# A wide S5 recurrence, a bound state copy, a diagonal skip on TensorE, and S5 outputs' DMAs on other queues

## Chip, cores and metric

One core of one Trainium2 chip runs the whole program in one launch. The metric is device time in microseconds (us), the median of the runs. Engines: TensorE (PE; PEld is its weight load), VectorE (DVE), ScalarE (ACT), GpSimd (POOL), SyncE (SP); SP's instructions are nearly all DMA issues.

## What is computed

Two layers of a hybrid block over 512 latent and 256 context tokens, width 1024. In each layer a token mixer joins three parts, then comes a gated FFN. The parts that the change touches, cut from the reference:

```python
def ssd_mixer(...):                       # width 256, 4 heads of 64
    y_l = d * x_l                         # the skip: d has one value per head
    for direction in range(2):
        yl_d, _ = ssd_scan(...)
        y_l = y_l + o(yl_d)
    return rmsnorm(y_l * silu(z_l), norm_w)

def s5_scan(u, ab, bb, h0):               # complex, 16 groups of 64 states, 16 channels a group
    h[t] = ab * h[t - 1] + bb @ u[t]      # written as an associative scan
def s5_mixer(...):                        # both directions, context then latent
    y = d * u + c_re @ h_re - c_im @ h_im
    y = gelu(y)
    return y * sigmoid(y @ glu_w + glu_b)
```

Differential attention (4 heads) is the third part. The last layer needs no outputs for the context tokens.

## The kernel before

Products in full precision are three fp32r products of high and low halves (L145 to L147). A layer runs its input products, the mixer (SSD, attention and S5 side by side), the output product and 22 blocks of the FFN. Each part is a Python generator, and the main function takes them forward in turns; a scheduler then fixes the order of instructions on each engine. An engine takes its own queue strictly in that order.

S5 works on chunks of 8 tokens: 96 chunks, 32 of the context and 64 of the latents. `SH` holds the states at the chunk borders, 128 partitions (64 states, forward on partitions 0 to 63, backward on 64 to 127) by real and imaginary part, 16 groups (2 x 8) and 96 columns. `s5_inputs` (L662) fills the columns with each chunk's own contribution, eight q at a time: SP loads of `Uq` (L699) and `Iq`, products (L677), ScalarE copies (L679 to L681). Then GpSimd runs the recurrence over the 96 columns, 95 steps of three instructions: L689 multiplies the last column by the powers of A (`s5t`), L691 adds the two halves (`s5u`), L692 adds that to the column. It is a generator, so SSD and attention work is queued between its steps.

`s5_outputs` (L702) runs over eight q. It loads `TO` (L708, L710) and `Uq` (L699) on SP, copies the states into `Iq` (VectorE L719 for the forward half, GpSimd L722 for the reversed one), multiplies (L726, L728), copies the result to `Yq` on ScalarE (L729) and stores it with SP (L731). `TO` and `Iq` have two buffers each. Then `gl` and `fu` are loaded (L738, L740), and the gelu, the gate's product (weights L752) and the gate follow.

In SSD, `scores` (L943) prepares one 128-token tile: GpSimd multiplies the tile by the skip weights (L976, `xdd`), VectorE adds that (L978) and the two directions (L979). `outputs` (L982) adds the within-chunk products (L986). `finish` (L990) gates, takes the reciprocal root of the mean square on GpSimd (L177 and L179, `rv` and `rr`), and scales by it on VectorE (L997). Layer 0 has six such tiles, layer 1 four.

Of the kernel before, what the change touches and what calls it, by code (L numbers as in the profile page):

```python
# [10 lines left out]
AF = mybir.ActivationFunctionType  # L11
# [13 lines left out]
NCH = CH_C + CH_L  # L25
# [30 lines left out]
HO = 1  # L56
F1 = 1
FL2 = 1
AE = 0
NB = 4  # L60
NM0 = 0
NM1 = 1
# [31 lines left out]
class Kern:  # L94
# [567 lines left out]
    def s5_inputs(self, l, P1):  # L662

        nc = self.nc

        SH = self.t(P1, [128, 2, 2, 8, NCH], "SH", bufs=1)
        self.SH = SH
        nc.gpsimd.memset(SH[:, :, :, :, 0:1], 0.0)
        for q in range(8):
# [12 lines left out]
            yield  # L682
        A = self.s5A[l].rearrange("p o i g q -> p o i (g q)")
        col = lambda k: SH[:, :, :, :, k].rearrange("p r g q -> p r (g q)")
        eng = nc.gpsimd
        yield
        for k in range(1, NCH):
            tt = self.sm(64, tag="s5t").rearrange("p (o i x) -> p o i x", o=2, i=2)
            eng.tensor_mul(tt, A, col(k - 1)[:, None].to_broadcast([128, 2, 2, 16]))  # L689
            u = self.sm(32, tag="s5u").rearrange("p (o x) -> p o x", o=2)  # L690
            eng.tensor_add(u, tt[:, :, 0], tt[:, :, 1])  # L691
            eng.tensor_add(col(k), col(k), u)  # L692
            if k % 5 == 0:
                yield

    def load_u(self, l, q, P1):
        U = self.t(P1, [128, 2, NCH], "Uq")
        for g in range(2):
            self.nc.sync.dma_start(U[:, g], self.ud[l][2 * q + g].rearrange("c j k -> j c k"))  # L699
        return U  # L700

    def s5_outputs(self, l, P1, P3, need_ctx):  # L702
# [99 lines left out]
    def ssd(self, l, P1, need_ctx):  # L802
# [99 lines left out]
        nc.tensor.matmul(cs[:, 1], self.m_ge, dA[:, :, 4:8], start=True, stop=True)  # L902
        tot = ps[:, 48:96].rearrange("p (d t h) -> p d t h", d=2, t=6)
        for d in range(2):
            nc.tensor.matmul(tot[:, d], self.ones, dA[:, :, d * 4:d * 4 + 4], start=True, stop=True)
        ac = self.t(P1, [128, 96], "acs", bufs=1)
        nc.scalar.copy(ac, ps[:, :96])
        eac = self.t(P1, [128, 2, 6, 4], "eac", bufs=1)
# [30 lines left out]
            yield  # L939
        toks = list(range(6 if need_ctx else TL))  # L940

        def scores(t):

            tok = slice(t * 128, (t + 1) * 128)
# [24 lines left out]
            for d in range(2):  # L969
                for g in range(2):  # L970
# [273 lines left out]
    def run(self):  # L1244
        tc, nc, I = self.tc, self.nc, self.I
        from contextlib import ExitStack
        with ExitStack() as es:
# [29 lines left out]
            self.ones = c([128, 128], "ones")  # L1277
            nc.vector.memset(self.ones, 1.0)
# [410 lines left out]
```

## Time and profile before

| | |
|---|---|
| median of 3 runs | 1928.36 us (1927.61 to 1930.28) |
| profiled execution | 1933.37 us, span 1931.6 us |
| busy: TensorE, VectorE, ScalarE, GpSimd | 1721.8, 1209.1, 735.6, 613.1 us |
| mean granted TensorE clock | 0.947 of full speed |

The span is the time from the first to the last instruction. A row of the busy time by window gives the window, its length, then the busy time (and instruction count) of PE, PEld, DVE, ACT and POOL, the granted TensorE clock, the DMA share and GB/s. A timeline row gives start, duration, engine, line, operation and tiles; what stands in brackets is the idle time of the engine before it and who ended it. A row of waits gives the sum, how many, and the longest. A price row gives the least, median and largest duration in ns, and the first and last start.

### The profile page before, as it was taken

Reading aid. Unit: us, or ns where it says so; the run is one execution under the profiler, and the core shown is the slowest. Engines: PE = TensorE matmul, PEld = TensorE weight load, DVE = VectorE, ACT = ScalarE, POOL = GpSimd, SP = SyncE. Lnnn points to the kernel's source line nnn. Section 1 sums busy time; section 2 is a strip of 40 time slices with the busy share of each in tenths; the row PEclk is TensorE's granted clock in tenths of the full one; section 3 lists DMA queues with packets and bytes.
Section 4 is the critical chain, followed back from the end, with each engine's and each line's share of the span. In section 5 each row is a group of like instructions: output and inputs, shape, how many; then the busy total and the mean of one; then the engine's idle time right before and its main releaser. Section 6 shows DMA issues by size and latency. Waiting matters only on the chain.

```text
span 1931.6 us, 26164 instructions
## 1 busy us (share of the span) xinstructions
PE 1721.8 (89%) x9485; PEld 1461.7 (76%) x9485; DVE 1209.1 (63%) x2212; ACT 735.6 (38%) x1375; POOL 613.1 (32%) x1027
## 2 busy tenths in 40 slices
PE   6989971886899899999999997998588999999998
PEld 1779861684788788888778887897477788888886
DVE  7877963875569456666556557657457464555555
ACT  3443420664444443322122235544346454232322
POOL 4436887120233644412600024088701210000002
PEclk8999995897999899999999998999799999999999
DMA  8464472454452333444533433452284343232322
GB/s 311 145 182 167 160 201 64 101 144 135 138 170 93 104 126 131 134 134 132 163 119 123 148 112 128 128 154 96 61 206 106 131 153 109 82 115 77 120 77 87
DMA packets 128818, 254.41 MB, mean 132 GB/s; under 512 B 42609, under 2 KB 65713, under 8 KB 128689
## 3 DMA queue, kind: packets, MB, share of 16 engines
q1 hardware_dynamic: 125312, 249.57, 41.5%
q10 hardware_dynamic: 3376, 3.17, 0.5%
q8 instruction: 75, 1.23, 0.3%
q14 instruction: 55, 0.44, 0.1%
HBM read 213.53 MB, written 41.16 MB: 132 GB/s over the span
## 4 chain that ended last, share of the span: by engine, by line
PE 49%; POOL 19%; DMA 11%; DVE 9%; issue 5%; ACT 4%; SPq 2%; POOLq 0%; DVEq 0%; ACTq 0%
POOL s5t L689 5%; PE pl L147 5%; PE pl L145 5%; PE pl L146 5%; POOL SH L692 4%; POOL s5u L691 4%; PE pc L146 3%; PE pc L147 3%; PE pc L145 3%; PE ma L145 3%; PE ma L146 3%; PE ma L147 3%; PE pp L146 3%; PE pp L145 3%; PE pp L147 3%
## 5 line engine op out<-in xcount | busy, mean ns | idle before, releaser
L140 DVE TENSOR_TENSOR lo<-raw,hi 128x1024 fp32r<-128x1024 f32 (+2 forms) x190 | 243.9, 1287 | 195.3 <-ACT hi L139 192.8
L139 ACT CAST hi<-raw 128x1024 fp32r<-128x1024 f32 (+2 forms) x190 | 197.4, 1042 | 440.2 <-PE pl L146 127.7
L147 PE MATMUL pl<-Hl,lo 128*128 128x512 f32 (+1 forms) x560 | 215.1, 384 | 10.0 <-DVE lo L140 10.0
L145 PE MATMUL pl<-Hl,hi 128*128 128x512 f32 (+1 forms) x560 | 215.6, 385 | 4.8 <-DVE xt L246 4.0
L177 POOL TENSOR_SCALAR rv<-ss 128x1 f32<-128x1 f32 x51 | 19.0, 373 | 629.0 <-ACT junk L185 627.0
L146 PE MATMUL pl<-Hl,hi 128*128 128x512 f32 (+1 forms) x560 | 214.1, 382 | 0.0
L1180 DVE TENSOR_TENSOR y<-y,ma 128x512 f32<-128x512 f32 x160 | 106.6, 683 | 87.4 <-PE ma L147 87.2
L145 PE MATMUL ma<-hi,ahi 128*128 128x512 f32 x360 | 141.7, 394 | 4.3 <-DVE y L1180 4.2
L146 PE MATMUL ma<-lo,ahi 128*128 128x512 f32 x360 | 140.8, 391 | 0.0
L147 PE MATMUL ma<-hi,alo 128*128 128x512 f32 x360 | 140.3, 390 | 0.0
L352 DVE SCALAR_TENSOR_TENSOR modj<-raw,crow 128x1024 bf16<-128x1024 f32 x56 | 72.6, 1297 | 92.9 <-DMA raw<-in_modw 92.5
L147 PEld LDWEIGHTS pl<-Hl,lo 128*128 128x128 f32 x560 | 107.0, 191 | 30.9 <-DVE lo L140 11.4
L145 PEld LDWEIGHTS pl<-Hl,hi 128*128 128x128 f32 x560 | 107.1, 191 | 23.9 <-issue 4.2
L692 POOL TENSOR_TENSOR SH<-SH,s5u 128x32 f32<-128x32 f32 x190 | 83.1, 438 | 126.5 <-ACT SH L680 112.1
L146 PEld LDWEIGHTS pl<-Hl,hi 128*128 128x128 f32 x560 | 107.2, 191 | 18.5
L145 PE MATMUL pp<-Hl,hi 128*128 128x512 f32 (+1 forms) x256 | 97.4, 383 | 13.8 <-ACT cvt L816 6.2
L145 PE MATMUL pc<-Hc,hi 128*128 128x256 f32 x352 | 99.7, 284 | 0.7 <-DVE de L395 0.7
L146 PE MATMUL pc<-Hc,hi 128*128 128x256 f32 x352 | 100.1, 284 | 0.2 <-DVE Hc L217 0.2
L147 PE MATMUL pc<-Hc,lo 128*128 128x256 f32 x352 | 99.8, 284 | 0.0
L146 PE MATMUL pp<-Hl,hi 128*128 128x512 f32 (+1 forms) x256 | 96.7, 378 | 0.5 <-DVE Hl L217 0.4
L147 PE MATMUL pp<-Hl,lo 128*128 128x512 f32 (+1 forms) x256 | 96.2, 376 | 0.5 <-DVE lo L140 0.5
L689 POOL TENSOR_TENSOR s5t<-s5A,SH 128x64 f32<-128x64 f32 x190 | 91.3, 481 | 14.3
(474 smaller groups left out, 4643.3 us busy)
## 6 DMA issues: line engine op xcount, KB each, us to landing
raw<-in_modw SPq DMA_DIRECT2D x56, 512.0 KB
raw<-in_wg SPq DMA_DIRECT2D x44, 512.0 KB
raw<-in_wu SPq DMA_DIRECT2D x44, 512.0 KB
raw<-in_wd SPq DMA_DIRECT2D x44, 512.0 KB
raw<-in_winf SPq DMA_DIRECT2D x28, 512.0 KB
modw<-in_modw SPq DMA_DIRECT2D x24, 512.0 KB
modw<-in_modwn SPq DMA_DIRECT2D x16, 512.0 KB
raw<-in_wout SPq DMA_DIRECT2D x16, 512.0 KB
```

The lines of the kernel that those rows point to most:

```text
L139: nc.scalar.copy(hi[:, :cols], raw[:, :cols])
L140: (eng or nc.vector).tensor_sub(lo[:, :cols], raw[:, :cols], hi[:, :cols].bitcast(F32))
L145: mm(out, lhs[0], rhs[0], start=first, stop=False)
L146: mm(out, lhs[0], rhs[1], start=False, stop=False)
L147: mm(out, lhs[1], rhs[0], start=False, stop=last)
L177: self.nc.gpsimd.tensor_scalar(v, ss, scale, eps, op0=ALU.mult, op1=ALU.add)
L352: ins = nc.vector.scalar_tensor_tensor(jk, w, 1.0, row[:, 0], op0=ALU.mult, op1=ALU.mult, accum_out=o[:, 0:1])
L689: eng.tensor_mul(tt, A, col(k - 1)[:, None].to_broadcast([128, 2, 2, 16]))
L691: eng.tensor_add(u, tt[:, :, 0], tt[:, :, 1])
L692: eng.tensor_add(col(k), col(k), u)
L1180: nc.vector.tensor_add(y[:, t, c], y[:, t, c], pb[h])
```

## The change

1. GpSimd's recurrence becomes wide. The powers A^2, A^4 and A^8 are made by 14 small instructions. Three levels up add neighbours at distances 1, 2 and 4 columns (`sweep`: one multiplication L709 and one addition L710 for each output part, input part and, where there are over 24 columns, half of the groups). A serial middle of 11 steps (columns 8, 16, ... 88) uses A^8, and three levels down fill the other columns. Per layer that is 64 wide instructions and 33 small ones where there were 285. The wide temporaries are `Iq` buffers.
2. The forward state copy (L753 now, L719 before) is bound to its place in program order on VectorE.
3. The skip is a product on TensorE: `DI`, the identity scaled by each head's weight (four ScalarE instructions per layer), times the tile, four 128x64 products that open `outputs`. The GpSimd product and the VectorE addition go. The sum over a chunk uses the two triangle masks in two products in place of a matrix of ones.
4. The S5 outputs' loads (TO, Uq, gl, fu, gate weights) are issued by GpSimd, their stores by ScalarE. `s5_inputs` keeps SP.

```diff
         for q in range(8):
-            U = self.load_u(l, q, P1)
+            U = self.load_u(l, q, P1, nc.sync)
...
-        for k in range(1, NCH):
+        def sweep(n, src, dst, m):
+            for o in range(2):
+                for i in range(2):
+                    w = 8 if m > 24 else 16
+                    for g in range(0, 16, w):
+                        x = slice(g, g + w)
+                        t = self.t(P1, [128, 2, 2, 128], "Iq", bufs=IQ).rearrange("p g r n -> p (g r n)")
+                        t = t[:, :w * m].rearrange("p (x k) -> p x k", x=w)
+                        eng.tensor_mul(t, X[:, i, x, src], AP[n][:, o ^ i, x, None].to_broadcast([128, w, m]))
+                        (eng.tensor_sub if o < i else eng.tensor_add)(X[:, o, x, dst], X[:, o, x, dst], t)
+                    yield
+        e = NCH
+        for n in range(3):
+            h = 1 << n
+            yield from sweep(n, slice(h, e - 2 * h, 2 * h), slice(2 * h, e, 2 * h), e // (2 * h) - 1)
+        for k in range(8, e, 8):
             tt = self.sm(64, tag="s5t").rearrange("p (o i x) -> p o i x", o=2, i=2)
-            eng.tensor_mul(tt, A, col(k - 1)[:, None].to_broadcast([128, 2, 2, 16]))
+            eng.tensor_mul(tt, A8, col(k - 8)[:, None].to_broadcast([128, 2, 2, 16]))
             u = self.sm(32, tag="s5u").rearrange("p (o x) -> p o x", o=2)
             eng.tensor_add(u, tt[:, :, 0], tt[:, :, 1])
             eng.tensor_add(col(k), col(k), u)
+        for n in reversed(range(3)):
+            h = 1 << n
+            yield from sweep(n, slice(0, e, 2 * h), slice(h, e, 2 * h), e // (2 * h))
...
-            nc.sync.dma_start(TO[:, :256].rearrange("p (g x) -> p g x", g=2), self.Td[l][:, 2 * q:2 * q + 2])
+            nc.gpsimd.dma_start(TO[:, :256].rearrange("p (g x) -> p g x", g=2), self.Td[l][:, 2 * q:2 * q + 2])
...
-            U = self.load_u(l, q, P1)
+            U = self.load_u(l, q, P1, nc.gpsimd)
...
-            ef(S[f, :, :, c0:], SH[f, :, :, q, c0:])
+            self.tc.keep_in_program_order(ef(S[f, :, :, c0:], SH[f, :, :, q, c0:]))
...
-                nc.sync.dma_start(self.yd[l][2 * q + g].rearrange("c j k -> j c k")[:, :, c0:], yb[:, g, c0:])
+                nc.scalar.dma_start(self.yd[l][2 * q + g].rearrange("c j k -> j c k")[:, :, c0:], yb[:, g, c0:])
...
-            sk = self.t(P1, [128, 256], "xdd")
-            nc.gpsimd.tensor_mul(sk, xB[:, t, :256], prm[:, 16:272])
-            ae = nc.gpsimd if AE else nc.vector
-            ae.tensor_add(yt[:, 1], yt[:, 1], sk)
-            ae.tensor_add(yt[:, 0], yt[:, 0], yt[:, 1])
+            nc.vector.tensor_add(yt[:, 0], yt[:, 0], yt[:, 1])
...
+            for h in range(4):
+                nc.tensor.matmul(yp[:, h * 64:(h + 1) * 64], DI[:, h], xB[:, t, h * 64:(h + 1) * 64], start=h == 0, stop=False)
```

VectorE in layer 0, where the state copy stood (`qkvt` is the rotary work of attention, `cv` and `gm` the SSD gates, `modj` the modulation). Before:

```order
L949 TENSOR_TENSOR gm_3628<-ma_3626,cst 128x512 [waits PE_49]
L352 SCALAR_TENSOR_TENSOR modj_3357,modc_112<-modw_3355,crow_1166 128x1024 [waits DMAHW4_49,DVE_49]
L1567 TENSOR_TENSOR qkvt_3586<-qkvt_3586,rope 128x512 [waits DMAHW7_49,DMAHW0_49,Activation_49]
L719 COPY Iq_4280<-SH_1369 64x384 [waits Pool_49]
L719 COPY Iq_4352<-SH_1369 64x384
L1566 TENSOR_TENSOR ropet_3588<-ropet_3588,rope 128x512 [waits Activation_49]
L965 TENSOR_TENSOR cv_3639<-cv_3639,gm_3628 128x512 [waits DVE_49,Activation_49]
```

And now, the same place, and, 26 rows behind L1602, the first row that waits for GpSimd:

```order
L988 TENSOR_TENSOR gm_3328<-ma_3326,cst 128x512 [waits PE_49]
L351 SCALAR_TENSOR_TENSOR modj_3019,modc_110<-modw_3017,crow_1164 128x1024 [waits DMAHW0_49,DVE_49]
L1602 TENSOR_TENSOR qkvt_3281<-qkvt_3281,rope 128x512 [waits DMAHW4_49,DMAHW3_49,Activation_49]
L1601 TENSOR_TENSOR ropet_3283<-ropet_3283,rope 128x512 [waits Activation_49]
L1004 TENSOR_TENSOR cv_3339<-cv_3339,gm_3328 128x512 [waits DVE_49,Activation_49]
...
L1031 SCALAR_TENSOR_TENSOR xdd_3592<-xdd_3592,z_1900 128x256 [waits DVE_49,Activation_49]
L1034 TENSOR_SCALAR yt_3357<-yt_3357,rr_665_3417 128x256 [waits Pool_49]
```

The two copies are gone from between the rotary work; the first stands 127 rows after L1602, among the output product's rows.

GpSimd in layer 1, around the first reciprocal root of the SSD. Before, it lies between steps of the recurrence:

```order
L692 TENSOR_TENSOR SH_11512<-SH_11512,s5u_12918 128x32 [waits Pool_49]
L177 TENSOR_SCALAR rv_2723_13232<-ss_13229 128x1 [waits Activation_49]
L689 TENSOR_TENSOR s5t_12921<-s5A_115,SH_11512 128x64 [waits Pool_49]
L179 TENSOR_TENSOR rr_2724_13234<-rv_2723_13232,mhalf 128x1 [waits Pool_49]
L691 TENSOR_TENSOR s5u_12923<-s5t_12921 128x32 [waits Pool_49]
```

And now, behind its last row, with the S5 outputs' loads after the four:

```order
L710 TENSOR_TENSOR SH_11218<-SH_11218,Iq_12838 128x384 [waits Pool_49]
L756 COPY Iq_13354<-SH_11218 64x4x64 [waits Pool_49]
L176 TENSOR_SCALAR rv_2444_12605<-ss_12602 128x1 [waits Activation_49,Pool_49]
L178 TENSOR_TENSOR rr_2445_12607<-rv_2444_12605,mhalf 128x1 [waits Pool_49]
...
L742 DMA TO_13347<-Td_81 128x256 [waits DMASW1_49,DVE_49,PE_49]
L744 DMA TO_13347<-Od_79 64x2x256 [waits DMASW2_49]
```

All four pairs of roots moved behind the recurrence and one copy.

GpSimd in layer 0, one q of the S5 outputs, where only the copies and the roots of attention (`oss`) were before:

```order
L733 DMA Uq_4111<-ud_72 128x1x96 [waits DMASW4_49,PE_49]
L733 DMA Uq_4111<-ud_72 128x1x96 [waits DMASW5_49]
L742 DMA TO_4107<-Td_80 128x256 [waits DMASW6_49,PE_49]
L744 DMA TO_4107<-Od_78 64x2x256 [waits DMASW7_49]
L744 DMA TO_4107<-Od_78 64x2x256 [waits DMASW0_49]
L756 COPY Iq_4114<-SH_1367 64x4x32 [waits DVE_49]
L756 COPY Iq_4114<-SH_1367 64x4x64
L176 TENSOR_SCALAR rv_892_4192<-oss_4026 128x2 [waits Activation_49,Pool_49]
```

Five loads per q stand in GpSimd's queue now, ahead of the copies and of attention's root.

## Rows read from the trace of the kernel before

**Rows 1.** The page: shares of the span of the chain that ended last, by engine.

```profile
PE 49%; POOL 19%; DMA 11%; DVE 9%; issue 5%; ACT 4%; SPq 2%; POOLq 0%; DVEq 0%; ACTq 0%
```

**Rows 2.** Busy time by window.

```profile
160.00:277.00 117.00, 114.08 (x793) 104.22 (x794) 101.72 (x212) 40.71 (x73) 103.80 (x166) 0.99 0.53 174
277.00:322.00 45.00, 0.83 (x2) 0.00 (x0) 0.29 (x2) 2.32 (x7) 35.86 (x122) 0.54 0.26 55
397.00:433.00 36.00, 33.61 (x254) 31.71 (x254) 29.84 (x65) 23.56 (x71) 11.02 (x19) 0.95 0.57 162
1255.00:1330.00 75.00, 73.70 (x523) 65.61 (x521) 53.26 (x130) 32.54 (x56) 63.26 (x148) 1.00 0.47 146
1330.00:1395.00 65.00, 38.61 (x234) 32.01 (x233) 27.46 (x49) 22.31 (x59) 53.73 (x150) 0.80 0.15 48
1396.00:1515.00 119.00, 103.55 (x654) 93.36 (x653) 78.75 (x139) 63.85 (x157) 9.39 (x14) 0.93 0.59 149
```

**Rows 3.** Timeline of POOL, three places.

```profile
160.28 0.67 POOL L692 TENSOR_TENSOR SH<-SH,s5u 128x32 f32<-128x32 f32 x1 [43.37 <-ACT SH L680]
...
321.95 6.03 POOL L722 COPY Iq<-SH 64x256 f32<-64x256 f32 x2
...
1255.23 0.28 POOL L692 TENSOR_TENSOR SH<-SH,s5u 128x32 f32<-128x32 f32 x1 [68.77 <-ACT SH L680]
```

**Rows 4.** Timeline of DVE in layer 0.

```profile
276.39 0.82 DVE L1567 TENSOR_TENSOR qkvt<-qkvt,rope 128x512 f32<-128x512 f32 x1
321.92 0.62 DVE L719 COPY Iq<-SH 64x384 f32<-64x384 f32 x2 [44.71 <-POOL SH L692]
...
344.13 0.35 DVE L997 TENSOR_SCALAR yt<-yt,rr 128x256 f32<-128x256 f32 x1
```

**Rows 5.** Waits of DVE from 1255 to 1420, of PE from 1320 to 1400.

```profile
DVE yt L997 <- POOL rr L179: 21.7, 4, 10.2
DVE yt L978 <- POOL xdd L976: 10.2, 1, 10.2
...
PE ma L1002 <- DVE yt L997: 17.0, 3, 7.8
PE ma L971 <- DVE gm L949: 6.7, 1, 6.7
```

**Rows 6.** Durations by line, ns min/median/max, over the whole span.

```profile
L689 POOL TENSOR_TENSOR s5t<-s5A,SH x190: 348/358/1418, 114.6 to 1391.0; 128x64 f32<-128x64 f32 x190
...
L691 POOL TENSOR_TENSOR s5u<-s5t x190: 250/253/1263, 115.8 to 1391.4; 128x32 f32<-128x32 f32 x190
...
L692 POOL TENSOR_TENSOR SH<-SH,s5u x190: 266/274/1352, 160.3 to 1392.1; 128x32 f32<-128x32 f32 x190
...
L601 POOL TENSOR_TENSOR s5x<-stag,stbg x20: 722/774/1822, 24.9 to 948.7; 128x256 f32<-128x256 f32 x20
...
L356 POOL TENSOR_TENSOR raw<-raw,crow x24: 2349/2407/3259, 576.1 to 799.0; 128x1024 f32<-128x1024 f32 x24
...
L986 PE MATMUL mb<-xdt,cv x160: 217/275/474, 323.8 to 1384.7; 128*128 128x64 f32 x160
```

**Rows 7.** Groups of POOL from 160 to 325.

```profile
L691 POOL TENSOR_TENSOR s5u<-s5t 128x32 f32<-128x32 f32 x94 | 40.7, 433 | 7.4
```

**Rows 8.** Timeline of DVE in layer 1.

```profile
1352.06 0.48 DVE L979 TENSOR_TENSOR yt<-yt 128x256 f32<-128x256 f32 x1
1362.77 0.35 DVE L997 TENSOR_SCALAR yt<-yt,rr 128x256 f32<-128x256 f32 x1 [10.23 <-POOL rr L179]
```

**Rows 9.** Durations of DMA issues by line, ns min/median/max.

```profile
L580 ACTq DMA_DIRECT2D Id<-s5is x8: 326/326/345, 67.2 to 95.2; - x8
...
L699 SPq DMA_DIRECT2D Uq<-ud x64: 574/597/738, 115.1 to 1469.5; - x64
...
L731 SPq DMA_DIRECT2D yd<-Yq x32: 572/596/650, 403.1 to 1480.8; - x32
```

**Rows 10.** The S5 output products of layer 1.

```profile
L728 PE MATMUL mb<-Iq,TO x64: 275/275/421, 1406.3 to 1479.5; 128*128 128x64 f32 x64
```

More of the change, by code (lines that the diff above doesn't have):

```diff
@@ L58 @@
 FL2 = 1
-AE = 0
 NB = 4
@@ L668, in s5_inputs @@
         nc.gpsimd.memset(SH[:, :, :, :, 0:1], 0.0)
+        eng = nc.gpsimd
+        A = self.s5A[l].rearrange("p o i g q -> p o i (g q)")
+        pw = self.t(P1, [128, 2, 2, 16], "s5pw", bufs=1)
+        A8 = self.t(P1, [128, 2, 2, 16], "s5A8", bufs=1)
+        AP = [A[:, :, 0], pw[:, 0], pw[:, 1]]
+        for a0, a1 in zip(AP, AP[1:] + [A8[:, :, 0]]):
+            t = self.sm(64, tag="s5t").rearrange("p (n x) -> p n x", n=4)
+            eng.tensor_mul(t[:, :2], a0, a0)
+            eng.tensor_sub(a1[:, 0], t[:, 0], t[:, 1])
+            eng.tensor_mul(t[:, 2], a0[:, 0], a0[:, 1])
+            eng.tensor_add(a1[:, 1], t[:, 2], t[:, 2])
+        eng.tensor_copy(A8[:, 1, 1], A8[:, 0, 0])
+        eng.tensor_scalar(A8[:, 0, 1], A8[:, 1, 0], -1.0, 0.0, op0=ALU.mult, op1=ALU.add)
         for q in range(8):
-            U = self.load_u(l, q, P1)
+            U = self.load_u(l, q, P1, nc.sync)
             Iq = self.t(P1, [128, 2, 2, 128], "Iq", bufs=IQ)
@@ L682, in s5_inputs @@
             yield
-        A = self.s5A[l].rearrange("p o i g q -> p o i (g q)")
-        col = lambda k: SH[:, :, :, :, k].rearrange("p r g q -> p r (g q)")
-        eng = nc.gpsimd
+        X = SH.rearrange("p r g q k -> p r (g q) k")
+        col = lambda k: X[:, :, :, k]
         yield
-        for k in range(1, NCH):
+        def sweep(n, src, dst, m):
[14 more added lines that the diff above has]
+        for k in range(8, e, 8):
             tt = self.sm(64, tag="s5t").rearrange("p (o i x) -> p o i x", o=2, i=2)
-            eng.tensor_mul(tt, A, col(k - 1)[:, None].to_broadcast([128, 2, 2, 16]))
+            eng.tensor_mul(tt, A8, col(k - 8)[:, None].to_broadcast([128, 2, 2, 16]))
             u = self.sm(32, tag="s5u").rearrange("p (o x) -> p o x", o=2)
@@ L692, in s5_inputs, with load_u @@
             eng.tensor_add(col(k), col(k), u)
-            if k % 5 == 0:
+            if k % 24 == 0:
                 yield
-    def load_u(self, l, q, P1):
+        for n in reversed(range(3)):
+            h = 1 << n
+            yield from sweep(n, slice(0, e, 2 * h), slice(h, e, 2 * h), e // (2 * h))
+    def load_u(self, l, q, P1, eng):
         U = self.t(P1, [128, 2, NCH], "Uq")
         for g in range(2):
-            self.nc.sync.dma_start(U[:, g], self.ud[l][2 * q + g].rearrange("c j k -> j c k"))
+            eng.dma_start(U[:, g], self.ud[l][2 * q + g].rearrange("c j k -> j c k"))
         return U
@@ L737, in s5_outputs @@
             y = self.t(P3, [128, Q, NCH], "gl", bufs=2)
-            nc.sync.dma_start(y[:, :, c0:], self.yd[l][i * 8:(i + 1) * 8].rearrange("g c j k -> (g c) j k")[:, :, c0:])
+            nc.gpsimd.dma_start(y[:, :, c0:], self.yd[l][i * 8:(i + 1) * 8].rearrange("g c j k -> (g c) j k")[:, :, c0:])
             u = self.t(P3, [128, Q, NCH], "fu")
-            nc.sync.dma_start(u[:, :, c0:], self.ud[l][i * 8:(i + 1) * 8].rearrange("g c j k -> (g c) j k")[:, :, c0:])
+            nc.gpsimd.dma_start(u[:, :, c0:], self.ud[l][i * 8:(i + 1) * 8].rearrange("g c j k -> (g c) j k")[:, :, c0:])
             yv, uv = y[:, :, c0:], u[:, :, c0:]
@@ L751, in s5_outputs @@
         gw = self.t(P3, [128, 2, 256], "gluw", bufs=1)
-        nc.sync.dma_start(gw, self.I["gluw"][l])
+        nc.gpsimd.dma_start(gw, self.I["gluw"][l])
         for m in range(2):
@@ L904, in ssd @@
         for d in range(2):
-            nc.tensor.matmul(tot[:, d], self.ones, dA[:, :, d * 4:d * 4 + 4], start=True, stop=True)
+            nc.tensor.matmul(tot[:, d], self.m_ge, dA[:, :, d * 4:d * 4 + 4], start=True, stop=False)
+            nc.tensor.matmul(tot[:, d], self.m_lt, dA[:, :, d * 4:d * 4 + 4], start=False, stop=True)
         ac = self.t(P1, [128, 96], "acs", bufs=1)
@@ L940, in ssd @@
         toks = list(range(6 if need_ctx else TL))
+        DI = self.t(P1, [128, 4, 128], "DI", bufs=1)
+        for h in range(4):
+            nc.scalar.activation(DI[:, h], self.ident, AF.Copy, scale=prm[:, 16 + h * 64:17 + h * 64])
         def scores(t):
@@ L974, in scores, with outputs @@
                                  eac[:, :, t, :, None].to_broadcast(shp))
-            sk = self.t(P1, [128, 256], "xdd")
-            nc.gpsimd.tensor_mul(sk, xB[:, t, :256], prm[:, 16:272])
-            ae = nc.gpsimd if AE else nc.vector
-            ae.tensor_add(yt[:, 1], yt[:, 1], sk)
-            ae.tensor_add(yt[:, 0], yt[:, 0], yt[:, 1])
+            nc.vector.tensor_add(yt[:, 0], yt[:, 0], yt[:, 1])
             return Es, xd, yt[:, 0]
-        def outputs(Es, xd, yt):
+        def outputs(t, Es, xd, yt):
             yp = self.bank("mb")
+            for h in range(4):
+                nc.tensor.matmul(yp[:, h * 64:(h + 1) * 64], DI[:, h], xB[:, t, h * 64:(h + 1) * 64], start=h == 0, stop=False)
             for d in range(2):
                 for h in range(4):
-                    nc.tensor.matmul(yp[:, h * 64:(h + 1) * 64], Es[d][:, h], xd[:, d, h], start=d == 0 and h == 0,
+                    nc.tensor.matmul(yp[:, h * 64:(h + 1) * 64], Es[d][:, h], xd[:, d, h], start=False,
                                      stop=d == 1 and h == 3)
@@ L1010, in ssd @@
             Es, xd, yt = live.pop(0)
-            outputs(Es, xd, yt)
+            outputs(t, Es, xd, yt)
             finish(t, yt)
@@ L1276, in run @@
             self.cosT, self.sinT = rope[:, 0], rope[:, 1]
-            self.ones = c([128, 128], "ones")
-            nc.vector.memset(self.ones, 1.0)
             self.mhalf = c([128, 1], "mhalf")
```

2 lines of the change are left out of this document (1 added, 1 removed).

## The prediction

> **What bounds the kernel now.** I began with the chain of work that ended last: TensorE holds 49% of it, but GpSimd holds 19% [rows 1], which is much for an engine that does the small work. The long work on it is the S5 recurrence, so I looked next at the stretches in which that runs, in the busy time by window [rows 2]. In layer 0 it begins at 160.28 [rows 3]; up to 277 TensorE is busy for 114.08 of 117 us, so it hides. From 277 to 322 TensorE does 0.83 us of 45 and VectorE 0.29, while GpSimd works on. The timeline of VectorE shows why [rows 4]: the last operation before is L1567 at 276.39, the next are the two state copies L719 at 321.92, after 44.71 us of waiting for the last L692. The copies are needed only by the S5 outputs, but VectorE takes its queue in order, and rotary, gate and mixer work that TensorE needs stands behind them.
>
> In layer 1 the recurrence begins at 1255.23 [rows 3]. There the copy does not come too early; what is late is small work that lies between steps of the recurrence in GpSimd's queue: the skip product L976 (10.2 us, once) and the reciprocal roots L179 (21.7 us in four waits) [rows 5]. From 1330 to 1395 TensorE is busy for 38.61 of 65 us only [rows 2], and its waits for VectorE's L997 and L949, which stand on this chain, make 17.0 + 6.7 = 23.7 us [rows 5].
>
> The prices are read against the profiled execution (1933.37 us, span 1931.6 us); it lies 5.0 us above the median of 1928.36 us. I apply the differences to the median.
>
> **The pin and the wide recurrence, layer 0.** The order (above) shows that both L719 are gone from behind L1567; the first state copy stands 127 rows later. VectorE's first wait on GpSimd is now 26 rows after that place, the scaling by `rr` (L1034; L997 before). The same operation ran at 344.13 before [rows 4], 22.2 us of VectorE's work after the stall. So the recurrence has until 277.2 + 22.2 = about 299 before anything is late again: 139 us from its start.
>
> What does it take? A column add of 128x32 costs 253 ns and the least price of a 128x256 add is 722 ns [rows 6], so an element costs (722 - 253)/224 = 2.09 ns and an instruction 186 ns. The wide levels, per layer: 16 x 376 elements, 16 x 384, 8 x 368, 8 x 384, 8 x 176 and 8 x 192, which is 15.6 + 15.8 + 7.6 + 7.9 + 4.4 + 4.7 = 56.1 us. The eleven middle steps cost 358 + 253 + 274 ns each [rows 6], 9.7 us. The levels 1 and 2 step through memory in 16 and 32 bytes: L692, with strided columns in and out, is 21 ns dearer than L691 for the same 32 elements, 0.66 ns per element, and on 8,960 elements of these levels that is 5.9 us (0 to 14 if none or all levels pay it). Gaps between dependent instructions: 7.4 us before 94 instructions, 79 ns each [rows 7], times 97 = 7.6 us. Sum 79 us free of disturbance. Disturbed it is more: from 160 to 277, beside a VectorE that is busy for 87%, 166 GpSimd instructions took 625 ns each; from 277 to 322, beside an idle one, 122 took 294 ns [rows 2]. I take this excess of 331 ns per instruction, not per element, because among the setup's 128x256 adds the median is 774 ns against a least 722, and the 128x1024 adds take 2407 against 2349 [rows 6]. 97 x 0.331 = 32 us, so 111 us, and the end is near 271, well ahead of 299. The layer's gain is the whole stall, **-44.7 us**. The 14 instructions for the powers of A run before the inputs are ready, in the 43.37 us in which GpSimd waited for ScalarE [rows 3]: nothing.
>
> [...]
>
> **Layer 1.** The excess beside VectorE is 63.26/148 = 427 ns less 294, 133 ns per instruction [rows 2], 13 us on 97: 92 us, and the end is near 1347. The order now has no rr inside the recurrence: all of them stand behind its last row and one copy, so the first is ready about 1348.5. The first is wanted when VectorE has done L979 (1352.06 + 0.48), less the 10.2 us of the skip wait that is gone: about 1342.3 [rows 8]. That leaves one wait of 6 us where 31.9 were; GpSimd is free for the others. TensorE's 23.7 us, three quarters of VectorE's 31.9, shrink with them to about 4. I take **-20 us**; ends -6 (excess per element, below) and -29 (no wait left, and TensorE at full clock instead of the 0.80 granted there [rows 2]).
>
> **The diagonal skip.** Ten products of 256 elements leave GpSimd (186 + 256 x 2.09 = 721 ns each by the price above) and ten adds leave VectorE (0.48 us each, as L979 of the same size [rows 8]): 4.8 us of VectorE, 2.9 of it with layer 0's six tokens, right behind the stall, where its queue is full. TensorE gets 40 matmuls of the shape of L986, 275 ns at most [rows 6], 11 us or less, in stages in which TensorE waits anyway. Four ScalarE scalings per layer are ready long before use. Net **-1 us**.
>
> **S5 loads on GpSimd.** Each q issues three loads of TO and two of U. The trace has no DMA issued by GpSimd, so the price is bounded: below by 326 ns, ScalarE's issue [rows 9], above by 1.4 us, the dearest small GpSimd instruction [rows 6]. SP takes 597 ns for the U loads [rows 9]; an engine that also computes and is disturbed beside VectorE adds the 0.33 us from above; I take 1.0 us. Two q are loaded ahead (TO has two buffers), so six q, 30 loads per layer, pace the stage. In layer 0 the q run within 397 to 433, and GpSimd already has 11.02 us of work there [rows 2]: 30 + 11 = 41 us in place of 36, and some landing behind TensorE's use of a buffer, as TensorE reads in order between attention products: **+8 us** (0 at 0.33 us, +17 at 1.4). In layer 1 the stage 1396 to 1515 is long (GpSimd 9.39 us [rows 2]; the S5 matmuls lie 73 us apart from first to last [rows 10]), so 30 + 9.4 us fit: 0. The U loads of the inputs stay on SP. SP loses some 45 issues per layer, and its transfers gain nothing on the chain.
>
> **Stores on ScalarE.** 16 per layer, 326 ns (its own issues) to 596 ns (SP's for these stores) [rows 9]: 5 to 10 us per layer on an engine that is busy for 23.56 of 36 us and 63.85 of 119 [rows 2]. Behind a store stand ScalarE's copies and exponentials that TensorE needs: **+2 us** (0 to 8).
>
> Sum: -44.7 - 20 - 1 + 8 + 2 = -55.7 us, so 1928.4 - 55.7 = **1873 us**.
>
> **Rivals.**
> (a) Cheap loads. If a GpSimd issue is as short as SP's, 30 x 0.6 + 11 = 29 us hides in 36, and the +8 vanishes; with the last 4 us of layer 1 won too, 1928.4 - 44.7 - 24 - 1 + 1 = 1860. For it: the free GpSimd time from 397 to 433. Against: an engine that computes is not SP.
> (b) Contention per element. If the factor 625/294 = 2.12 holds for wide operations, layer 0's recurrence reaches 299 with 9 us of free work left and ends near 309: -34. Layer 1, by 427/294 = 1.45, ends near 1367, so VectorE waits 25 us at the first rr: -6. Sum -31, 1897. For it: two state copies of 64x256 elements that took 6.03 us beside a VectorE that had just gone on [rows 3]; against: the medians of the wide adds.
> (c) Slower: GpSimd's DMA issues as the bound. Its queue holds copies, rr for attention and the loads; TensorE takes S5 and attention products in one order, so a late load stops both. With a price p the two stages need 60p + 20.4 us against 36 + 73 = 109; the remaining terms give -63.7, so it decides from p = 2.5 us. At 3.0 us, what each of those two copies took [rows 3], it would be 91 - 64 = +28, 1956 us. Against: such a price stands in one pair of copies; GpSimd's 19 instructions from 397 to 433 average 0.58 us [rows 2].
> [...] The chance of (c) stands on the two copies alone.
>
> **How the numbers follow.** Forecast 0.56, (a) 0.20, (b) 0.16, (c) 0.05, something else 0.03. The range goes from 1848 (as (a), with layer 1's -29 and the stage gaining from SP's relief) to 1899 (past (b)); outside lie (c) and the tails. 0.2%, 3.9 us, is what a measurement can tell from no change. All cases but (c) are far on the faster side: faster 0.93, within 0.2% 0.02, slower 0.05.
>
> **What would show it.** Right: no VectorE wait on the recurrence in layer 0; GpSimd's last wide operation near 271; wide adds near 1.0 to 1.4 us; in layer 1 one rr wait under 10 us and TensorE above 38 us busy in some 45; GpSimd issues near 1 us and q 5 to 7 us apart in layer 0. Wrong: wide operations of 2 us, VectorE waiting at L1034 in layer 0, TensorE waiting on TO or U for more than 15 us in a layer, or a ScalarE exponential behind a store that TensorE waits for.

## The result, and the profile after

The changed kernel takes 1943.95 us (median of 4 runs, 1941.68 to 1947.60), the kernel before 1929.32 us in the same comparison: the ratio is 1.0082, 95% interval 1.0065 to 1.0099. It is slower by 15 us, where 55 us less were forecast. Times in this document are medians of the undisturbed runs: one of the six of pin_skip, 3398.74 us, is left out. The profiled execution took 1941.68 us (span 1939.9 us), 8.3 us more than that of before, so the traces show a little over half of the difference between the medians.

The chain of the page has changed as forecast. GpSimd's 19% [rows 1] are 5%:

```profile
PE 44%; DMA 12%; DVE 11%; POOL 5%; ACT 4%; issue 4%; SPq 0%; ACTq 0%; POOLq 0%; DVEq 0%
```

So the recurrence is nearly off the path, and the kernel is slower all the same. The busy time by window of the changed kernel shows both (columns as in [rows 2]):

```profile
160.00:264.00 104.00, 86.73 (x542) 78.38 (x542) 98.93 (x143) 28.25 (x52) 99.64 (x95) 0.89 0.37 123
264.00:304.00 40.00, 38.63 (x249) 34.52 (x250) 36.78 (x72) 11.32 (x18) 0.98 (x2) 0.91 0.55 187
...
1262.00:1345.00 83.00, 69.81 (x458) 61.79 (x456) 64.09 (x100) 27.54 (x49) 79.76 (x95) 0.94 0.37 111
```

The wide recurrence runs from 161 to 264 and from 1262 to 1347. Beside it VectorE is busy for 98.93 of 104 us with 143 instructions; before, it did 212 in 101.72 of 117 us [rows 2]. TensorE, at 114.08 of 117 us in that stretch before, has 86.73 of 104. There is no stall of 45 us any more, but the stretch itself has slowed down.

A ledger over the program shows where the time went. Each stage is the time between two events that every trace has (the first or last start of a group of instructions), in us:

| stage | before | changed | no_levels | no_dma | pieces | halves |
|---|---|---|---|---|---|---|
| start to last S5 input product, layer 0 | 156.7 | 157.5 | 157.7 | 157.0 | 157.3 | 157.1 |
| a: to VectorE's last rotary product | 119.7 | 146.3 | 117.2 | 146.5 | 122.5 | 139.1 |
| b: to the first SSD transposition | 68.1 | 29.5 | 25.0 | 23.5 | 45.5 | 25.3 |
| c: to the first S5 output product | 52.5 | 53.5 | 54.3 | 55.5 | 54.6 | 54.7 |
| d: to the last attention product, layer 0 | 117.3 | 134.0 | 136.6 | 116.1 | 117.7 | 114.6 |
| e: to the last S5 input product, layer 1 | 738.4 | 738.5 | 744.0 | 738.3 | 739.9 | 738.5 |
| f: to the last SSD transposition, layer 1 | 140.9 | 140.4 | 120.0 | 141.5 | 138.2 | 138.2 |
| g: to the last attention product, layer 1 | 117.3 | 120.4 | 120.1 | 109.2 | 108.5 | 110.1 |
| h: to the end | 420.7 | 419.8 | 421.5 | 421.1 | 419.7 | 421.9 |

The first two columns say it: b gives 38.6 us, a takes 26.6, d takes 16.7, g takes 3.1, and f, where 31.9 us of VectorE's waits are gone, gives 0.5. The other columns are experiments told below.

What happens in a and f is seen in VectorE's groups of instructions beside the recurrence (shape by shape: count, then busy us, mean ns, then idle before). First the kernel before, from 161 to 277:

```profile
L352 DVE SCALAR_TENSOR_TENSOR modj<-modw,crow 128x1024 bf16<-128x1024 f32 x19 | 23.9, 1259 | 4.3 <-DMA modw<-in_modw 4.2
...
L937 DVE SCALAR_TENSOR_TENSOR Hin<-Hin,et,ma 128x64 f32<-128x64 f32 x20 | 4.9, 269 | 0.0
...
L1017 DVE TENSOR_TENSOR xdt<-xB,dt 128x256 f32<-128x256 f32 x10 | 4.7, 505 | 0.0
...
L1566 DVE TENSOR_TENSOR ropet<-ropet,rope 128x512 f32<-128x512 f32 x5 | 3.9, 773 | 0.3 <-ACT ropet L1565 0.3
```

and the changed kernel, from 161 to 264:

```profile
L351 DVE SCALAR_TENSOR_TENSOR modj<-modw,crow 128x1024 bf16<-128x1024 f32 x10 | 19.3, 1930 | 0.0
...
L1054 DVE TENSOR_TENSOR xdt<-xB,dt 128x256 f32<-128x256 f32 x8 | 6.8, 891 | 0.0
...
L1601 DVE TENSOR_TENSOR ropet<-ropet,rope 128x512 f32<-128x512 f32 x3 | 4.1, 1353 | 0.0
...
L972 DVE SCALAR_TENSOR_TENSOR Hin<-Hin,et,ma 128x64 f32<-128x64 f32 x8 | 1.9, 269 | 0.0
```

The modulation sums (L352, now L351) went from 1259 to 1930 ns, a 256-element product (L1017, now L1054) from 505 to 891, a rotary product from 773 to 1353. The state update L937 (now L972), which has one operand in PSUM, stayed at 269. The timeline shows the pattern. These are VectorE's operations of 48 elements:

```profile
185.27 0.92 DVE L394 TENSOR_SCALAR cvt<-cvt 128x48 f32<-128x48 f32 x1
186.22 0.90 DVE L385 TENSOR_SCALAR cvt<-cvt 128x48 f32<-128x48 f32 x1
187.16 0.90 DVE L387 TENSOR_SCALAR cvt<-cvt 128x48 f32<-128x48 f32 x1
188.09 1.09 DVE L388 TENSOR_SCALAR cvt<-cvt 128x48 f32<-128x48 f32 x1
189.22 0.21 DVE L397 SCALAR_TENSOR_TENSOR cvt<-cvt 128x48 f32<-128x48 f32 x1
```

and GpSimd's wide ones beside them (two to a row):

```profile
184.15 1.99 POOL L710 TENSOR_TENSOR SH<-SH,Iq 128x376 f32<-128x376 f32 x2
186.09 1.93 POOL L709 TENSOR_TENSOR Iq<-SH,s5pw 128x368 f32<-128x368 f32 x2
187.98 2.47 POOL L710 TENSOR_TENSOR SH<-SH,Iq 128x368 f32<-128x368 f32 x2
```

VectorE's first four rows last 0.9 to 1.1 us, the length of one wide GpSimd operation, where the last one lasts 0.21. The same four took 0.19 to 0.30 us in the kernel before. Here VectorE gets one operation through for each of GpSimd's, and GpSimd's are hardly longer for it: 0.97 to 1.23 us, at most 7% above the least of each shape (0.991, 0.967 and 1.155). Beside VectorE's long modulation sums they are: two wide additions, of 0.99 us each at the least, took

```profile
169.24 3.95 POOL L710 TENSOR_TENSOR SH<-SH,Iq 128x376 f32<-128x376 f32 x2
```

So in these rows the two engines take turns: a VectorE operation of 0.2 to 0.3 us lasts as long as GpSimd's of 1 us, and an addition of 0.99 us takes 2.00 beside sums of 1.73 to 1.92. What makes them take turns the traces do not show.

### The profile page after: what moved, and what is told of

Its sections match the earlier page's. It is cut to its first block, busy times and chain, and to the rows that moved or that the text cites. A ratio compares the mean times of both kernels' runs of the same rounds, so it can differ in the third digit from the quotient of the medians.

```text
span 1939.9 us, 26032 instructions
## 1 busy us (share of the span) xinstructions
PE 1746.6 (90%) x9573; PEld 1483.3 (76%) x9573; DVE 1264.6 (65%) x2201; ACT 738.4 (38%) x1383; POOL 595.2 (31%) x759
## 3 DMA queue, kind: packets, MB, share of 16 engines
q8 instruction: 75, 1.23, 0.3%
## 4 chain that ended last, share of the span: by engine, by line
PE 44%; DMA 12%; DVE 11%; POOL 5%; ACT 4%; issue 4%; SPq 0%; ACTq 0%; POOLq 0%; DVEq 0%
DMA raw<-in_modw 4%; PE pl L146 4%; PE pl L144 4%; PE pl L145 4%; PE ma L144 3%; PE ma L145 3%; PE ma L146 3%; PE pc L145 3%; PE pc L146 3%; PE pc L144 3%; DVE lo L139 3%; PE pp L145 2%; PE pp L144 2%; PE pp L146 2%; POOL raw L355 2%
## 5 line engine op out<-in xcount | busy, mean ns | idle before, releaser
L146 PE MATMUL ma<-hi,alo 128*128 128x512 f32 x360 | 140.4, 391 | 0.0
L351 DVE SCALAR_TENSOR_TENSOR modj<-raw,crow 128x1024 bf16<-128x1024 f32 x56 | 74.1, 1324 | 92.5 <-DMA raw<-in_modw 91.0
L144 PE MATMUL pp<-Hl,hi 128*128 128x512 f32 (+1 forms) x256 | 100.4, 395 | 15.8 <-ACT cvt L850 5.8
L145 PE MATMUL pp<-Hl,hi 128*128 128x512 f32 (+1 forms) x256 | 99.7, 390 | 0.2
L144 PE MATMUL pp<-hi,Hl 128*128 128x256 f32 (+1 forms) x256 | 90.0, 356 | 6.9 <-DVE xt L249 4.8
L145 PE MATMUL pp<-lo,Hl 128*128 128x256 f32 (+1 forms) x256 | 88.9, 348 | 1.8 <-DVE lo L139 1.7
```

The source lines that it names most:

```text
L144: mm(out, lhs[0], rhs[0], start=first, stop=False)
L145: mm(out, lhs[0], rhs[1], start=False, stop=False)
L146: mm(out, lhs[1], rhs[0], start=False, stop=last)
L351: ins = nc.vector.scalar_tensor_tensor(jk, w, 1.0, row[:, 0], op0=ALU.mult, op1=ALU.mult, accum_out=o[:, 0:1])
```

## Experiments

Theory 1: GpSimd's long operations and VectorE's hold each other up, and VectorE is the one on the path. Theory 2: the S5 outputs' DMAs in the queues of GpSimd and ScalarE cost what the stall gave. The first four kernels undo or isolate these.

**no_levels**

```diff
-        for n in range(3):
+        for n in range(0):
...
-        for n in reversed(range(3)):
+        for n in reversed(range(0)):
```

> The changed kernel without its six wide levels (the 64 wide GpSimd instructions per layer are left out, so the S5 part is not computed; the rest stays). Theory 1 (GpSimd's wide operations and VectorE's hold each other up): layer 0's last rotary product on VectorE comes back from 303.8 us to 278 or earlier, VectorE's modulation sums back from 1.93 and 1.68 us mean to about 1.26, and the time falls by some 25 us in each layer, to about 1897 us (1885 to 1910). Theory 2 (the S5 outputs' DMAs on GpSimd and ScalarE are what costs): the time falls by less than 10 us, to 1935 to 1944.

Measured: 1891.1 us (ratio to the kernel before 0.979, 0.976 to 0.982). The last rotary product came at 274.9; the busy time of that stage:

```profile
157.00:275.00 118.00, 114.77 (x806) 105.17 (x804) 97.55 (x224) 42.29 (x73) 21.05 (x35) 0.99 0.52 172
```

VectorE is busy for 97.55 us; with the levels the same stretch of work takes it 137.75 us (no_dma, 157 to 304, shown at the end). In the ledger a falls by 29.1 us and f by 20.4. Theory 1 holds: the levels cost 53 us of the whole (1943.95 - 1891.13), where 47 were expected. (The profiled run is the slowest of its four, so the ledger shows 43.5 of them.) d does not fall, so something else is at work there.

Stage f, first in the changed kernel, then without the levels; VectorE's 184 instructions take 104.56 and 74.74 us:

```profile
1259.30:1399.70 140.40, 119.73 (x810) 105.33 (x808) 104.56 (x184) 56.11 (x118) 90.24 (x111) 0.93 0.33 100
```

```profile
1234.80:1354.80 120.00, 114.47 (x811) 102.18 (x810) 74.74 (x184) 56.48 (x118) 19.52 (x47) 0.98 0.38 118
```

**no_dma**: loads and stores of the S5 outputs back on SyncE.

```diff
-            U = self.load_u(l, q, P1, nc.gpsimd)
+            U = self.load_u(l, q, P1)
...
-                nc.scalar.dma_start(self.yd[l][2 * q + g]...)
+                nc.sync.dma_start(self.yd[l][2 * q + g]...)
```

> The changed kernel with the S5 outputs' loads and stores back on SyncE. Theory 2: the S5 output stage of layer 0 is back from 60 to about 37 us, layer 1's from 82 to about 73, and the time is 1912 to 1922 us. Theory 1 alone: the time stays within 6 us of 1944.

Measured: 1911.4 us (0.9905, 0.987 to 0.994), 32.6 us less than the changed kernel and faster than the kernel before. In the ledger d goes back from 134.0 to 116.1 and g from 120.4 to 109.2; a and f stay. Theory 2 holds as well, beside theory 1.

**dma_alone**: that part of the diff alone, in the kernel before.

> The kernel before, with only the S5 outputs' loads on GpSimd and stores on ScalarE. Theory 2: the stages get 9 and 23 us longer, 1950 to 1960 us in all. Theory 1: 1926 to 1934 us.

Measured: 1941.4 us (1.0056, 1.0037 to 1.0075). The DMAs cost 12 us here, a third of the 32.6 us in the changed kernel and less than expected. The cost depends on the rest of the program; on what in it was not settled.

**pin_alone**

```diff
-            ef(S[f, :, :, c0:], SH[f, :, :, q, c0:])
+            self.tc.keep_in_program_order(ef(S[f, :, :, c0:], SH[f, :, :, q, c0:]))
```

> The kernel before, with only VectorE's state copy bound to its place. The narrow recurrence takes little from VectorE (theory 1), so the stall shrinks to the wait of the first SSD tiles for the skip product and the reciprocal root: 44.7 us become 20 to 35, and the time is 1908 to 1920 us. If the wait for the recurrence only changes its place, 1926 to 1932 us.

Measured: 1919.1 us (0.9935, 0.991 to 0.996), at the upper end of what was expected. Two new waits of VectorE in layer 0 have taken most of the 44.7 us:

```profile
DVE yt L997 <- POOL rr L179: 19.6, 1, 19.6
DVE yt L978 <- POOL xdd L976: 18.5, 1, 18.5
```

The next four kernels look into both costs.

**pieces**: no_dma with every wide operation cut into four.

```diff
-                    w = 8 if m > 24 else 16
+                    w = 2 if m > 24 else 4
```

> The changed kernel with its DMAs back on SyncE (as no_dma) and every wide operation cut into four (94 or 96 elements where there were 376 or 384, 44 or 48 where there were 176 or 192): 256 short operations per layer for 64. In no_dma VectorE was busy for 137.75 us from 157 to 304, without the levels 97.55 us, so 64 wide operations cost it 40 us. If the loss goes by the operation (each one holds VectorE up once), it grows to 100 us or more and the last rotary product of layer 0 comes after 340 us. If it goes by elements, it stays near 40 us and the product near 303. If only long operations make VectorE wait, and short ones wait themselves (as the narrow recurrence of before seems to do), it falls under 20 us and the product comes before 290; then the recurrence is slower (256 x 0.7 us, ends near 350) and the time is 1915 to 1935.

Measured: 1906.7 us (0.988, 0.985 to 0.991). The last rotary product came at 279.8, the third of the expected cases: in layer 0 the same elements in short operations hold VectorE up far less. Its modulation sums:

```profile
L352 DVE SCALAR_TENSOR_TENSOR modj<-modw,crow 128x1024 bf16<-128x1024 f32 x14 | 18.6, 1326 | 1.0 <-DMA modw<-in_modw 1.0
```

The recurrence is longer for it (it ends near 323, where 350 was expected), and layer 0 pays that at the first root:

```profile
DVE yt L1035 <- POOL rr L179: 18.9, 2, 17.9
```

Layer 1 shows no such relief. Stage f gains 3.3 us on no_dma (141.5 to 138.2), and VectorE is busy in it for 103.51 us, as long as with whole operations (102.86 in no_dma):

```profile
1237.50:1375.70 138.20, 121.76 (x811) 107.16 (x809) 103.51 (x184) 55.80 (x118) 125.66 (x296) 0.93 0.33 103
```

**halves**: the same with `w = 4 if m > 24 else 8`.

> As pieces, but every wide operation cut in two (188 or 192 elements, 88 or 96): 128 operations per layer. Pieces (256) took 1906.7 us, with the last rotary product of layer 0 at 279.8; no_dma (64) 1911.4 us, with it at 303.5. If VectorE's wait grows steadily with the length of one GpSimd operation, it lies between, near 290, and VectorE is busy for 10 to 25 us more than without the levels; the recurrence then ends earlier than in pieces and the time is 1898 to 1908. If any operation above some length under 188 elements costs the full price, the product is at 300 or later and the time 1908 to 1916.

Measured: 1905.2 us (0.9875, 0.985 to 0.990). The rotary product came at 296.2, a little later than the 290 expected, between pieces and no_dma, and the same sums between theirs:

```profile
L352 DVE SCALAR_TENSOR_TENSOR modj<-modw,crow 128x1024 bf16<-128x1024 f32 x12 | 18.5, 1541 | 0.4 <-DMA modw<-in_modw 0.4
```

So in layer 0 the price of such a sum grows steadily with the length of one GpSimd operation (1231 ns without the levels, 1326 at 94 to 96 elements, 1541 at 188 to 192, 1930 at 376 to 384). The wait at the root is short again, 0.9 us.

Layer 1 again shows none of it: VectorE is busy for 105.55 us of stage f. Nearly half of its loss there is one operation, which takes 1.2 us at the least:

```profile
1250.33 15.20 DVE L140 TENSOR_TENSOR lo<-raw,hi 128x1024 fp32r<-128x1024 f32 x1 [1.61 <-ACT hi L139]
```

Beside it GpSimd ran 30 operations of 0.38 to 0.67 us, each begun before the one ahead had ended. VectorE's ended 1 us after the first gap, 0.08 us long, and now GpSimd's next one was the long one, 1.28 us:

```profile
1264.07 0.38 POOL L710 TENSOR_TENSOR Iq<-SH,s5pw 128x88 f32<-128x88 f32 x1
1264.53 1.28 POOL L711 TENSOR_TENSOR SH<-SH,Iq 128x88 f32<-128x88 f32 x1
```

TensorE waited 14.3 us for that operation. Pieces has two such places in layer 1 (5.69 and 4.82 us). In layer 0 VectorE gets its turn without such a gap: in the changed kernel GpSimd's wide operations follow each other without one from 161.2 to 204.5, and the modulation sums that start from 164.8 to 177.9 take 1.37 to 2.02 us. What decides it was not settled.

Halves is faster than the kernel before and than the changed one. That cutting the operations makes the whole kernel faster than no_dma is not shown, for halves or for pieces; the intervals overlap.

**loads_gp**: the changed kernel with only the stores back on SyncE.

> The changed kernel with only the S5 outputs' stores back on SyncE; the loads stay on GpSimd. No_dma gained 32.6 us on the changed kernel. If the loads are the cost (their latency behind TensorE's use of the two buffers), at most 10 us come back: 1934 to 1944. If the stores on ScalarE are (0.59 us each ahead of its copies and exponentials), 20 or more: 1912 to 1924.

Measured: 1933.9 us (1.0025, 1.0005 to 1.0046): 10.0 us for the stores, at the upper end of what the first case expected.

**stores_act**: the changed kernel with only the loads back on SyncE.

> The changed kernel with only the S5 outputs' loads back on SyncE; the stores stay on ScalarE. The loads as the cost: 1911 to 1920. The stores as the cost: 1932 to 1944.

Measured: 1923.4 us (0.998, 0.996 to 0.9998), 12.0 us above no_dma and 20.5 below the changed kernel; this lies between the two cases. Loads make about two thirds of the 32.6 us, stores one third, and within the noise they add up.

**pin_skip**: the kernel before with the pin and the skip on TensorE.

> The kernel before with the bound copy and the skip on TensorE, the narrow recurrence and all DMAs as before. In pin_alone the two waits of layer 0 (18.5 for the skip product, 19.6 for the root) both end with the recurrence; without the product they become one of some 35 us, so the same time as pin_alone, 1914 to 1922. If the skip itself saves VectorE and GpSimd work on the path, 1905 to 1913.

Measured: 1916.4 us (0.993, 0.990 to 0.995), as the first case expected. The interval overlaps that of pin_alone, so a gain by the skip alone is not shown.

**pin_wide**: the kernel before with the pin and the wide recurrence.

> The kernel before with the bound copy and the wide recurrence only (no_dma without the skip on TensorE). If the skip is worth little, 1909 to 1915 us as no_dma. If it matters that the skip product no longer stands behind GpSimd's wide operations, the time is 1918 or more.

Measured: 1918.1 us (0.9946, 0.992 to 0.997). Against pin_alone's 0.9935 the wide recurrence by itself is worth nothing. Together with the skip (no_dma) it is 6.7 us faster. The time is at the edge of the second case, but its reason is not shown: the intervals of pin_wide and no_dma overlap, and in the trace of pin_wide VectorE never waits for the skip product.

**uq_gp** and **to_gp**: stores on SyncE, and only some loads on GpSimd.

> The changed kernel with the stores and the three loads of TO back on SyncE; only Uq, gl, fu and the gate's weights are loaded by GpSimd (20 of its 44 loads per layer). All loads on GpSimd (loads_gp) cost 22.5 us against no_dma. If the cost is that of a load waiting for its buffer ahead of GpSimd's copies and other loads (the Uq load is the one that waits for TensorE), most of it stays: 1924 to 1934. If it goes by the number of issues or by the landing of TO, which TensorE was seen to wait for, under half stays: 1911 to 1922.

> The counterpart of uq_gp: only the three loads of TO per q are issued by GpSimd (24 per layer). The wait of a Uq load as the cost: 1911 to 1918. Issues or the landing of TO as the cost: 1921 to 1934.

Measured: 1922.6 us (0.997, 0.995 to 0.998) and 1922.8 us (0.997, 0.995 to 0.9995), each 11 us above no_dma; this is just above the second case of the one and in the second case of the other. Neither a Uq load's wait nor TO's landing alone is the cause; each half of the loads costs half.

**loads_act**: the loads issued by ScalarE.

```diff
-            U = self.load_u(l, q, P1, nc.gpsimd)
+            U = self.load_u(l, q, P1, nc.scalar)
```

> As loads_gp (wide recurrence, pin, skip, stores on SyncE), but the S5 outputs' loads are issued by ScalarE in place of GpSimd. On SyncE they gave 1911.4 us, on GpSimd 1933.9. If it is GpSimd's way of issuing (landing in 5 to 6 us) that costs, ScalarE's loads cost little: 1911 to 1921. If it is that the loads stand in the queue of an engine that also computes, in order with its own work and waits, they cost as much as on GpSimd or more: 1928 to 1945.

Measured: 1930.8 us (1.0022, 1.0009 to 1.0035), nearly as slow as from GpSimd (the intervals overlap). So the loads cost 19.4 us on no_dma in ScalarE's queue and 22.5 in GpSimd's, two engines that also compute; that GpSimd's own way of issuing adds anything (3 us by the medians, under 1 by the ratios) is not shown.

The issues themselves are short. Duration of one in the changed kernel, ns least, median, largest:

```profile
L733 POOL DMA_DIRECT2D Uq<-ud x32: 582/624/837, 152.9 to 1477.0; - x32
...
L742 POOL DMA_DIRECT2D TO<-Td x16: 580/592/652, 379.4 to 1477.6; - x16
...
L765 ACTq DMA_DIRECT2D yd<-Yq x32: 579/590/1169, 398.7 to 1496.0; - x32
```

That is 0.59 to 0.62 us, as SyncE's for the `Uq` loads and the stores [rows 9]; SyncE's for `TO<-Td` took 0.40 at the median in the kernel before. What differs on a computing engine is the order: the loads stand between its own work. One q of GpSimd's queue in layer 0:

```profile
410.18 0.63 POOL L756 COPY Iq<-SH 64x128 f32<-64x128 f32 x2
415.03 1.24 POOL L733 DMA_DIRECT2D Uq<-ud  x2 [4.22 <-PE mb L760]
416.26 0.59 POOL L742 DMA_DIRECT2D TO<-Td  x1
416.84 1.20 POOL L744 DMA_DIRECT2D TO<-Od  x2
418.03 0.65 POOL L756 COPY Iq<-SH 64x128 f32<-64x128 f32 x2
```

The loads stood 4.22 us for TensorE to release a buffer of an earlier q, and the copy for this q stood behind them. TensorE's larger waits in stage d of the changed kernel, and those of no_dma (sum, how many, longest):

```profile
PE pp L1121 <- ACT p L1127: 11.1, 6, 3.5
PE ma L1149 <- ACT wT L1150: 5.8, 2, 2.9
PE mb L760 <- DMA TO<-Td: 3.7, 2, 2.2
```

```profile
PE pp L1122 <- ACT p L1128: 8.8, 5, 3.8
PE pp L1122 <- DMA Hc<-kd: 6.4, 1, 6.4
PE ma L1154 <- ACT wT L1151: 2.8, 4, 1.3
...
PE mb L761 <- DMA TO<-Td: 0.6, 1, 0.6
```

And the busy time of that stage, first the changed kernel, then no_dma:

```profile
386.80:520.80 134.00, 100.03 (x565) 86.36 (x564) 77.14 (x150) 63.75 (x162) 36.76 (x63) 0.86 0.42 115
```

```profile
382.50:498.60 116.10, 93.21 (x566) 78.89 (x565) 76.53 (x149) 63.40 (x162) 14.90 (x27) 0.91 0.48 138
```

TensorE's waits on softmax, on transposed weights and on TO are longer (one wait of no_dma, 6.4 us on an attention operand, is gone), and its granted clock is 0.86 where no_dma has 0.91; 565 matmuls take 100.03 us where 566 took 93.21. Of the 17.9 us between the two, 6.8 are longer matmuls and the rest is idle time. How much of the idle time is the queue's waiting and how much the other order that the scheduler gave the attention products around it was not separated.

## Why the prediction was wrong, point by point

**The stall and the recurrence's length: right, the length in part by luck.** VectorE no longer waits for the recurrence in layer 0. The last wide operation ends at 264.0 (forecast 271) and, in layer 1, at 1346.8 (forecast 1347, from a start 7 us earlier):

```profile
260.32 3.68 POOL L710 TENSOR_TENSOR SH<-SH,Iq 128x384 f32<-128x384 f32 x2
...
1343.64 3.14 POOL L710 TENSOR_TENSOR SH<-SH,Iq 128x384 f32<-128x384 f32 x2
```

The excess of 331 ns for each instruction was not what happened: some wide operations paid nothing, and the 16 multiplications by A in layer 0 took 822 ns at the least and 1808 at the median. Among my signs of being wrong stood "wide operations of 2 us", and some came.

**Layer 1's waits: right in themselves.** VectorE's idle time before the roots is down from 21.7 us [rows 5], over all of the program:

```profile
  POOL rr L178: 2.1, 3
```

**The step that failed: "beside a VectorE that is busy for 87%, 166 GpSimd instructions took 625 ns each".** I read the contention from GpSimd's side only. I charged the recurrence 32 us for it and VectorE nothing, without a reason. The narrow recurrence of before had indeed slowed VectorE little: 104.05 us busy from 157 to 277, 97.55 us without the levels. A narrow operation lasts 0.25 to 0.36 us at the median [rows 6], a wide addition 1.20 (0.67 to 2.14). Wide operations cost VectorE 40 us of busy time in layer 0, of which 27 to 29 us were on the path (stage a), and 30 us in layer 1, of which 20 were on the path (stage f); there they ate the whole gain. The missing term is about +47 us. Rival (b) asked about contention too, but again only for GpSimd's time.

The sum should have had a term on both sides. The traces of layer 0 show both: GpSimd's additions of 2.00 us where the least is 0.99, VectorE's operations of 0.9 to 1.1 us that took 0.19 to 0.30 before, and a mean modulation sum of 1930 ns that came back to 1326 when GpSimd's operations were cut to a quarter. The state update, with an operand in PSUM, took 269 ns before and after; why it was not longer was not shown. Layer 1 shows more than one operation waited out: in halves VectorE's of 15.20 us had 30 GpSimd instructions beside it.

**The S5 outputs' DMAs: the price was too high and the cost too low.** I took 1.0 us a load's issue and got +8 us, and +2 for the stores. A load's issue is 0.62 us, and yet the loads cost 20 to 23 us and the stores 10 to 12 in the changed kernel. The working counted the engine's time per q against the stage's length. What it left out is that loads, copies and roots wait in one order, some of them for TensorE, and that TensorE's granted clock was lower: 0.86 in stage d with 34 us of idle time, 0.91 with 23 (no_dma). That the order makes the cost is argued from these rows; the other order of the attention products came with it, and the two were not separated. Rival (c) had the place right and the mechanism wrong: it asked for 2.5 us an issue. Rival (a), that issues are as short as SyncE's, came true but for `TO<-Td` (0.59 us, SyncE's 0.40) and brought nothing.

**What came next after the stall: not asked.** In the 45 us of before, loads went on while VectorE and TensorE stood (55 GB/s from 277 to 322 [rows 2]): attention operands that follow landed while nobody worked, and TensorE waits for no DMA from 277 to 345. Now TensorE meets them (timeline of TensorE in layer 0):

```profile
323.11 1.22 PE L1121 MATMUL pp<-k,q 128*128 128x512 f32 x2 [12.49 <-DMA Hc<-qd]
```

The kernels without the stall all have such a wait (10.0 us in no_levels, 8.9 in no_dma, 7.8 in halves). It is part of why b gave 38.6 us and not 44.7.

**The skip: not settled.** It was forecast at -1 us; the medians give -6.7 by no_dma against pin_wide and -2.7 by pin_skip against pin_alone, and in both pairs the intervals overlap.

**The sum from the runs.** From the kernel before, in medians of their comparisons: pin and wide recurrence -11, skip -7, stores on ScalarE +12, loads on GpSimd +21: +15 us, the result. Each term is the step from one measured kernel to the next, so the sum has to close; in another order the terms differ (all DMAs together cost 12 us in dma_alone). The forecast's sum, with 47 us for VectorE put in and 33 for 10 at the DMAs, comes to +14.

## What to carry to other kernels

Where GpSimd works beside VectorE, count the time that each of its long operations takes from VectorE as well as the other way round: here the levels, nearly off the path, took 40 us of VectorE's busy time in layer 0 and 53 us of the whole. Short operations took less from VectorE in layer 0 (1326 ns a modulation sum beside 94 to 96 elements, 1930 beside 376 to 384), but in layer 1 one VectorE operation lasted 15.20 us beside 30 of them without gaps (halves), so read the trace after cutting. A DMA moved to an engine that computes can cost more than a price per issue says (here 20 to 23 us for the loads at 0.62 us an issue, where 1.0 us an issue had given 8): read what stands in front of it and behind it in that queue, and what each waits for. Before you bank the whole of a stall, look at what landed during it: here TensorE waited 12.49 us for a load once the stall was gone.

## What the runs showed that was not expected

In layer 0 the loss of VectorE grows with the length of a single GpSimd operation, not with GpSimd's busy time, and in layer 1 it does not (104.56 us busy in the changed kernel, 105.55 in halves, 103.51 in pieces). Layer 0, first pieces, then no_dma: in pieces GpSimd is busy for 140.18 us of 157 to 304, in no_dma for 100.81, and still VectorE has its last rotary product 24 us earlier in pieces.

```profile
157.00:304.00 147.00, 128.71 (x872) 116.09 (x870) 129.91 (x250) 50.53 (x96) 140.18 (x225) 0.94 0.60 178
```

```profile
157.00:304.00 147.00, 127.52 (x802) 114.00 (x801) 137.75 (x220) 42.30 (x73) 100.81 (x97) 0.88 0.42 139
```

Adds with a larger step of the addresses took longer. The in-place adds of level 0 (8-byte steps, 376 elements) and of level 1 (16-byte steps, 368 elements) in layer 1, ns least, median, largest:

```profile
L710 POOL TENSOR_TENSOR SH<-SH,Iq x8: 991/1020/1478, 1263.7 to 1277.7; 128x376 f32<-128x376 f32 x8
...
L710 POOL TENSOR_TENSOR SH<-SH,Iq x4: 1155/1197/2144, 1280.6 to 1288.0; 128x368 f32<-128x368 f32 x4
```

The least is 991 ns for the one and 1155 for the other, 17% more for 2% fewer elements; less the forecast's 186 ns an instruction it is 23% more per element, an estimate. Their shapes differ as well (8 rows of 47 and 16 of 23), so how much of it is the step was not shown.
